# State additions between convolution taps, gate projections cut in halves, step sizes by 128-column weights

## The chip, the cores and the metric

The kernel runs on one core of a Trainium2 chip. The metric is the device time of one execution in microseconds (us). Engines are named as in the profile: PE (TensorE matmuls), PEld (its weight loads), DVE (VectorE), ACT (ScalarE), POOL (GpSimd), SP (the queue that issues DMAs). Each engine works through its own queue strictly in order.

## The reference, cut to what matters

One layer on 512 latent tokens and 256 context tokens, with D = 1024 and 32-bit inputs. Two branches read the same normalized input `h`: a retention branch with four heads, and a state-space branch (SSD) with eight groups of four heads.

```
xbc = silu(dwconv_centred(xbc, conv_w, conv_b))          # five taps over time
xs, bm, cm = split(xbc)
dt = softplus(dt_raw + dt_bias)                          # step sizes, 64 columns of h @ w_in
a  = dt * -exp(a_log)
# per direction, chunk by chunk, starting from the context's final state:
y  = q.S * exp(cumsum a) + intra-chunk part
S' = exp(sum a) * S + sum_j k_j (to_end * v_j)           # "fade" and "gain"
ys = (y + D*xs) * silu(z)                                # z: a gate projection
out = (sigmoid(g_r) * o_ret + sigmoid(g_s) * o_ssd) @ w_out
```

## The kernel before, in words

All projections are 32-bit products made of three passes (`mm3`): input and weight are each split into a high part (`hh`, `whi`) and a residue (`hl`, `wlo`), and high x high, residue x high and high x residue are added in PSUM. A weight unit (128 x 1024, eight contraction tiles of 128 columns) is loaded by SP, cast by ACT (`cast`, or L126 in `wunit`) and its residue taken by DVE (`rest`, or L127).

The kernel has four stages: modulation and normalization (to about 76 us), retention (to about 500 us), the state-space branch (to about 985 us), and the output projections.

**Retention** is ordered by a scheduler. For each head: queries, keys and values (`qkv`), `attention`, a gate projection (`gproj`), a norm, and `finish` (transposes at L418, products with the gate at L420). Between the values of head 1 and `finish` of head 0 the step sizes are computed (`stepsizes`): a projection of 64 columns onto 512 and then 256 tokens, copied from PSUM by ACT, then a long run of DVE steps (softplus, cumulative sums, decays). Those DVE steps stand in DVE's queue among the score products of head 1's attention (`a` at L368, its residue `al` at L155, which PE needs at L380).

**The state-space branch** is written in a fixed order. Eight groups overlap: while group g is scanned (`cur`), group g+1's inputs are projected (`job`), so the loop starts at g = -1 with projections alone. A group has six slots, one weight unit each: s = 0 to 3 are convolution inputs (x0, x1, B, C), s = 4 and 5 are the two gate projections (z). In slot s PE runs the projection of this slot while DVE applies the convolution of the job of the slot before (`prev.taps`, four products with `scalar_tensor_tensor` at L645 behind a first tap on ACT, then `prev.finish` at L650). The scan of the current group is woven in:

- `turn`, `turned`: transposes of x and B on PE (L725), their copies on ACT, weighted values `vw` on DVE (L740). Tiles 4 and 5 are the context, in slot 4; tiles 0 and 3 follow in slot 5.
- `context_state` (slot 5): the context's state, on PE (L746), copied by ACT.
- `fade(i)` (POOL, L765) multiplies a state by its decay, `gain(i)` (PE, L755) makes what one chunk adds, and `gained(i)` (DVE, L759) adds the two. So the states are a chain: fade(0), gained(0), fade(1), gained(1), fade(2), gained(2).
- `readers` (POOL, L794), `exponents` (POOL, L777), `choose` (DVE, L781), `weigh` (DVE, L789): the scan's decay factors.
- `outputs(0)` at the start of slot 3, `outputs(1)` at the start of slot 4 (PE, L808) read the four states. `merge` (DVE, L816 and L817) takes their results.

Of the kernel before, what the change touches and what calls it, by code (L numbers as in the profile page):

```python
# [7 lines left out]
F32 = mybir.dt.float32  # L8
# [57 lines left out]
def hybrid_layer_kernel(ctx: ExitStack, tc: tile.TileContext, x, xc, vec, tab, msk, w_mod, bgate, npost,  # L66
# [63 lines left out]
    def mm3(ps, pairs):  # L130

        n = len(pairs)
        for i, (a, b) in enumerate(pairs):
            ah, al = a
            bh, bl = b
            nc.tensor.matmul(ps, ah, bh, start=(i == 0), stop=False)  # L136
            nc.tensor.matmul(ps, ah, bl, start=False, stop=False)  # L137
            nc.tensor.matmul(ps, al, bh, start=False, stop=(i == n - 1))  # L138
# [132 lines left out]
    with ExitStack() as st:  # L271
# [151 lines left out]
        def stepsizes():  # L423
# [3 lines left out]
            wk = projw(wunit(w_dt), 64)  # L427
            u = t("dtu")
            ps = bank([64, LT])
            proj(ps, wk, 0, LT)  # L430
            nc.scalar.copy(u[0:64, :], ps[:, 0:384])
            nc.scalar.copy(u[64:128, 0:128], ps[:, 384:512])
            ps = bank([64, LC])
            proj(ps, wk, LT, LC)
            nc.scalar.copy(u[64:128, 128:384], ps)
# [13 lines left out]
            m = t("dtm")  # L449
# [135 lines left out]
    with ExitStack() as st:  # L585
# [25 lines left out]
        class Conv:  # L611
# [27 lines left out]
            def taps(self):  # L639
# [4 lines left out]
                for i in range(1, 5):  # L644
                    nc.vector.scalar_tensor_tensor(acc, raw[:, i:i + n], col(w0 + i), acc, ALU.mult, ALU.add)  # L645
# [6 lines left out]
        class Gate:  # L652
# [5 lines left out]
            def mm(self, wk, part):  # L658
                if part == 0:
                    self.pa = pbank("pr", 3)  # L660
                    proj(self.pa, wk, 0, LT)
# [14 lines left out]

            def finish(self):
                pass

        class Late:  # L680


            def __init__(self, job):
                self.early = self.taps = self.finish = lambda: None
# [160 lines left out]
        def slot(s, t, job, prev, old, cur, nxt):  # L845
# [14 lines left out]
            elif s == 1:  # L860
# [7 lines left out]
                call(cur, ("readers", 1), ("decay", 2), ("gained", 1), ("fade", 2), ("decay", 3))  # L868
                rest(t + 2)
                prev.finish()  # L870
                call(cur, ("weigh", 2), ("weigh", 3))
            elif s == 2:
# [7 lines left out]
                call(cur, ("readers", 2), ("readers", 3), ("gained", 2))  # L880
                rest(t + 2)
                prev.finish()
            elif s == 3:
# [5 lines left out]
                cast(t + 2)  # L889
                rest(t + 2)  # L890
                prev.finish()
                call(old, ("totalled",))
            elif s == 4:
                call(cur, ("outputs", 1))
                prev.early()
                call(nxt, ("open",), ("turn", 4, 5))
                job.mm(w, 0)
                prev.taps()
                cast(t + 2)
# [4 lines left out]
            elif s == 5:  # L904
                prev.early()
                call(nxt, ("context_state",))
                job.mm(w, 0)
# [5 lines left out]
            else:  # L913
                prev.early()
                job.mm(w, 0)
                cast(t + 2)
# [284 lines left out]
```

## Time and profile before

| | us |
|---|---|
| median of three timed runs | 1286.09 (1284.51 to 1289.94) |
| profiled execution, its own time | 1284.94 |
| span of that execution | 1283.2 |

The profiled execution lies 1.15 us under the median, and 1.74 us of it lie outside the span. By engine, PE has matmuls in flight in 96% of the span and DVE is busy in 63%; but DVE's share is an average over unequal stages: in slices 17 to 30 of 40, which is the state-space branch, it is 70 to 90% and more, while it is mostly 20 to 70% elsewhere. A matmul's listed duration covers its way through the array, so back-to-back matmuls overlap and the distance between starts is what each costs. PE's idle time is therefore read from the waits and from stretches, not from the busy sum.

### The profile page before, as it was taken

Reading aid. Unit: us, or ns where it says so; the run is one execution under the profiler, and the core shown is the slowest. Engines: PE = TensorE matmul, PEld = TensorE weight load, DVE = VectorE, ACT = ScalarE, POOL = GpSimd, SP = SyncE. Lnnn points to the kernel's source line nnn. Section 1 sums busy time; section 2 is a strip of 40 time slices with the busy share of each in tenths; the row PEclk is TensorE's granted clock in tenths of the full one; section 3 lists DMA queues with packets and bytes.
Section 4 is the critical chain, followed back from the end, with each engine's and each line's share of the span. In section 5 each row is a group of like instructions: output and inputs, shape, how many; then the busy total and the mean of one; then the engine's idle time right before and its main releaser. Section 6 shows DMA issues by size and latency. Waiting matters only on the chain.

```text
span 1283.2 us, 16075 instructions
## 1 busy us (share of the span) xinstructions
PE 1232.5 (96%) x6415; PEld 1011.7 (79%) x6415; DVE 814.5 (63%) x951; ACT 436.8 (34%) x694; POOL 335.4 (26%) x272
## 2 busy tenths in 40 slices
PE   5899999899999999999999999999999999999997
PEld 1588888688888888788888878787878888888876
DVE  1774442963454254879998998998984347344543
ACT  2533232233323212434344434344333443222221
POOL 0330110101011000365554756574553200000000
PEclk9899999999999999999999999999999999999999
DMA  8431122122202214315253442525153466345521
GB/s 311 171 96 48 66 66 66 54 79 79 82 33 82 66 50 156 147 50 199 72 190 112 151 156 95 188 72 197 54 210 99 156 205 215 115 147 164 203 93 65
DMA packets 43100, 155.92 MB, mean 122 GB/s; under 512 B 5097, under 2 KB 5897, under 8 KB 37906
## 3 DMA queue, kind: packets, MB, share of 16 engines
q1 hardware_dynamic: 42322, 152.77, 34.5%
q0 software_dynamic: 704, 2.13, 0.7%
q8 instruction: 50, 0.82, 0.3%
q14 instruction: 24, 0.20, 0.1%
HBM read 144.10 MB, written 10.78 MB: 121 GB/s over the span
## 4 chain that ended last, share of the span: by engine, by line
PE 80%; DVE 12%; issue 2%; ACT 1%; DMA 0%; DVEq 0%; POOLq 0%; ACTq 0%
PE pj L136 12%; PE pj L138 11%; PE pj L137 11%; PE pb L342 7%; PE pr L136 7%; DVE cacc L645 6%; PE pr L138 6%; PE pr L137 6%; PE py L808 4%; PE pj L342 3%; PE pj L1072 2%; PE pb L1072 2%; PE pb L380 2%; PE pb L378 1%; PE pb L379 1%
## 5 line engine op out<-in xcount | busy, mean ns | idle before, releaser
L136 PE MATMUL pr<-hh,whi 128*128 128x512 f32 (+1 forms) x640 | 240.2, 375 | 0.0
L138 PE MATMUL pr<-hh,wlo 128*128 128x512 f32 (+1 forms) x640 | 229.6, 359 | 0.0
L137 PE MATMUL pr<-hl,whi 128*128 128x512 f32 (+1 forms) x640 | 229.3, 358 | 0.0
L127 DVE TENSOR_TENSOR wlo<-wraw,whi 128x1024 fp32r<-128x1024 f32 x89 | 108.8, 1223 | 165.8 <-ACT whi L126 165.6
L126 ACT CAST whi<-wraw 128x1024 fp32r<-128x1024 f32 x89 | 93.7, 1053 | 247.3 <-PE pj L137 155.6
L645 DVE SCALAR_TENSOR_TENSOR cacc<-raw,vt,cacc 128x772 f32<-128x772 f32 x96 | 138.6, 1444 | 11.3 <-ACT cacc L643 7.8
L136 PE MATMUL pj<-hh,whi 128*128 128x512 f32 (+3 forms) x384 | 142.2, 370 | 0.0
L138 PE MATMUL pj<-hh,wlo 128*128 128x512 f32 (+3 forms) x384 | 142.1, 370 | 0.0
L137 PE MATMUL pj<-hl,whi 128*128 128x512 f32 (+3 forms) x384 | 142.1, 370 | 0.0
L136 PEld LDWEIGHTS pr<-hh,whi 128*128 128x128 f32 x640 | 121.1, 189 | 20.1 <-issue 3.5
L137 PEld LDWEIGHTS pr<-hl,whi 128*128 128x128 f32 x640 | 121.2, 189 | 18.7 <-issue 1.9
L138 PEld LDWEIGHTS pr<-hh,wlo 128*128 128x128 f32 x640 | 121.0, 189 | 18.3
L777 POOL TENSOR_TENSOR rows<-rows,ctok 128x512 f32<-128x512 f32 x64 | 89.5, 1420 | 108.5 <-DMA rows<-rows_d 105.2
L794 POOL TENSOR_TENSOR rows<-c,rows 128x512 f32<-128x512 f32 x64 | 112.5, 1782 | 0.0
L559 DVE TENSOR_TENSOR wlo<-wraw,whi 128x1024 fp32r<-128x1024 f32 x56 | 89.2, 1594 | 19.2 <-ACT whi L552 19.2
L137 PE MATMUL pj<-ul,whi 128*128 128x512 f32 x256 | 100.7, 393 | 0.0
L136 PE MATMUL pj<-uh,whi 128*128 128x512 f32 x256 | 100.7, 393 | 0.0
L138 PE MATMUL pj<-uh,wlo 128*128 128x512 f32 x256 | 100.6, 393 | 0.0
L136 PEld LDWEIGHTS pj<-hh,whi 128*128 128x128 f32 (+1 forms) x384 | 71.7, 187 | 13.2 <-issue 0.2
L138 PEld LDWEIGHTS pj<-hh,wlo 128*128 128x128 f32 (+1 forms) x384 | 71.8, 187 | 12.9
L137 PEld LDWEIGHTS pj<-hl,whi 128*128 128x128 f32 (+1 forms) x384 | 71.6, 187 | 12.9
L649 ACT ACTIVATE cth<-cacc 128x772 f32<-128x772 f32 (+1 forms) x32 | 25.4, 795 | 146.9 <-DVE cacc L645 146.9
(280 smaller groups left out, 2178.5 us busy)
## 6 DMA issues: line engine op xcount, KB each, us to landing
rows<-rows_d SPq DMA_DIRECT2D x32, 1024.0 KB, 7.5
wmod<-in_w_mod_dram SPq DMA_DIRECT2D x8, 1024.0 KB, 8.7
wraw<-in_w_v_dram SPq DMA_DIRECT2D x16, 512.0 KB, 3.5
wraw<-in_w_g_dram SPq DMA_DIRECT2D x16, 512.0 KB
wraw<-in_w_xs_dram SPq DMA_DIRECT2D x16, 512.0 KB, 3.5
wraw<-in_w_z_dram SPq DMA_DIRECT2D x16, 512.0 KB, 3.4
wraw<-in_w_gt_dram SPq DMA_DIRECT2D x16, 512.0 KB, 3.7
uraw<-u_d SPq DMA_DIRECT2D x32, 256.0 KB, 3.6
```

Source lines behind the costliest of these rows:

```text
L126: nc.scalar.copy(hi, raw)
L127: (eng or nc.vector).tensor_tensor(lo, raw, hi.bitcast(F32), ALU.subtract)
L136: nc.tensor.matmul(ps, ah, bh, start=(i == 0), stop=False)
L137: nc.tensor.matmul(ps, ah, bl, start=False, stop=False)
L138: nc.tensor.matmul(ps, al, bh, start=False, stop=(i == n - 1))
L342: nc.tensor.matmul(pv[i], a[:, k, sl], wv[b][:, k2, :], start=(k == 0 and j == 0), stop=(k == KT - 1 and j == 2))
L559: nc.vector.tensor_tensor(lo, r, hi.bitcast(F32), ALU.subtract)
L645: nc.vector.scalar_tensor_tensor(acc, raw[:, i:i + n], col(w0 + i), acc, ALU.mult, ALU.add)
L777: nc.gpsimd.tensor_tensor(v64(rows[:, d, :]), v64(rows[:, d, :]), bc(cb, 3, 64), ALU.add)
L794: nc.gpsimd.tensor_tensor(rows[:, 2 + d, :], self.c2, rows[:, 2 + d, :], ALU.mult)
L808: nc.tensor.matmul(py[64 * q:64 * q + 64, sl], lhs, rhs, start=(term == 0), stop=(term == 2))
L1072: nc.tensor.matmul(pss[e], mg[k][a][:, sl], wo[k][b][:, ec], start=(k == 0 and j == 0), stop=(k == KT - 1 and j == 2))
```

## The change

Three edits.

1. `taps` is cut in two: `taps` issues taps 1 and 2, the new `taps2` taps 3 and 4. In slots 1 and 2 `gained(1)` and `gained(2)` now stand on DVE between the two halves. In slots 3 and 4 both halves follow each other as before, with `cast` on ACT between them in slot 3.
2. The gate projections of slots 4 and 5 (and of the last stretch) are issued as two halves of four contraction tiles each, in one PSUM accumulation. In slot 4 the first half stands ahead of the context's transposes, in slot 5 ahead of `context_state`; the second half stands behind.
3. `stepsizes` puts the high part and the residue of its 64 columns side by side as one 128-column weight. Two passes (with `hh` and `hl`) replace three; the two halves of the result are copied apart by six ACT copies instead of three and added on DVE. The cast and the residue cover 512 columns instead of 1024.

```diff
-            wk = projw(wunit(w_dt), 64)
+            nc.scalar.copy(bv[:, :, 0:64], rv)
+            nc.vector.tensor_tensor(bv[:, :, 64:128], rv, bv[:, :, 0:64].bitcast(F32), ALU.subtract)
             u = t("dtu")
-            ps = bank([64, LT])
-            proj(ps, wk, 0, LT)
-            nc.scalar.copy(u[0:64, :], ps[:, 0:384])
-            nc.scalar.copy(u[64:128, 0:128], ps[:, 384:512])
-            ps = bank([64, LC])
-            proj(ps, wk, LT, LC)
-            nc.scalar.copy(u[64:128, 128:384], ps)
+            u2 = t("dtm")
+            for t0, n, parts in ((0, LT, ((0, 0, 384, 0), (64, 384, 512, 0))), (LT, LC, ((64, 0, LC, 128),))):
+                ps = bank([P, n])
+                for k in range(KT):
+                    for h in (hh, hl):
+                        nc.tensor.matmul(ps, bv[:, k, :], h[:, k, t0:t0 + n], start=(k == 0 and h is hh),
+                                         stop=(k == KT - 1 and h is hl))
+                for p0, a0, a1, c0 in parts:
+                    nc.scalar.copy(u[p0:p0 + 64, c0:c0 + a1 - a0], ps[0:64, a0:a1])
+                    nc.scalar.copy(u2[p0:p0 + 64, c0:c0 + a1 - a0], ps[64:128, a0:a1])
+            nc.vector.tensor_tensor(u, u, u2, ALU.add)
...
-                for i in range(1, 5):
+                for i in range(1, 3):
+                    nc.vector.scalar_tensor_tensor(acc, raw[:, i:i + n], col(w0 + i), acc, ALU.mult, ALU.add)
+
+            def taps2(self):
+                n, raw, acc, w0 = self.n, self.raw, self.acc, V_CW + self.ctile * 5
+                for i in range(3, 5):
                     nc.vector.scalar_tensor_tensor(acc, raw[:, i:i + n], col(w0 + i), acc, ALU.mult, ALU.add)
...
             def mm(self, wk, part):
                 if part == 0:
                     self.pa = pbank("pr", 3)
-                    proj(self.pa, wk, 0, LT)
+                half = slice(4 * part, 4 * part + 4)
+                mm3(self.pa, list(zip(wk, hsl(0, LT)))[half], part == 0, part == 1)
...
                 call(cur, ("readers", 1), ("decay", 2), ("gained", 1), ("fade", 2), ("decay", 3))
+                prev.taps2()
                 rest(t + 2)
...
                 call(cur, ("readers", 2), ("readers", 3), ("gained", 2))
+                prev.taps2()
                 rest(t + 2)
...
                 prev.early()
+                job.mm(w, 0)
                 call(nxt, ("open",), ("turn", 4, 5))
-                job.mm(w, 0)
+                job.mm(w, 1)
...
                 prev.early()
+                job.mm(w, 0)
                 call(nxt, ("context_state",))
-                job.mm(w, 0)
+                job.mm(w, 1)
```

DVE in slots 1 and 2 of one group, before (`cacc` is the convolution, `st` the state with `tk` from PE, `wlo` the residue of a weight unit, `rows` the decay factors):

```order
L740 TENSOR_TENSOR vw<-tk,wtok 128x512 x2
L645 SCALAR_TENSOR_TENSOR cacc<-raw_3645,vt,cacc 128x772 x4
L759 TENSOR_TENSOR st_4388<-st_4388,tk 128x512
L559 TENSOR_TENSOR wlo<-wraw,whi 128x1024
L650 SCALAR_TENSOR_TENSOR x_4509<-cth,cacc 128x772
L789 TENSOR_TENSOR rows<-rows,sc 128x512 x2
L645 SCALAR_TENSOR_TENSOR cacc<-raw_3646,vt,cacc 128x772 x4
L759 TENSOR_TENSOR st_4389<-st_4389,tk 128x512
```

The same place after:

```order
L759 TENSOR_TENSOR vw<-tk,wtok 128x512 x2
L656 SCALAR_TENSOR_TENSOR cacc<-raw_3632,vt,cacc 128x772 x2
L778 TENSOR_TENSOR st_4388<-st_4388,tk 128x512
L661 SCALAR_TENSOR_TENSOR cacc<-raw_3632,vt,cacc 128x772 x2
L570 TENSOR_TENSOR wlo<-wraw,whi 128x1024
L666 SCALAR_TENSOR_TENSOR x_4496<-cth,cacc 128x772
L808 TENSOR_TENSOR rows<-rows,sc 128x512 x2
L656 SCALAR_TENSOR_TENSOR cacc<-raw_3633,vt,cacc 128x772 x2
L778 TENSOR_TENSOR st_4389<-st_4389,tk 128x512
L661 SCALAR_TENSOR_TENSOR cacc<-raw_3633,vt,cacc 128x772 x2
```

Each state addition has moved ahead of two of the four taps of its slot; the number of instructions is the same.

PE in slot 4 of the first pass (g = -1), before, around the context's transposes (`tk<-ident`); the 24 matmuls of the gate follow them:

```order
L138 MATMUL pr<-hh,wlo 128x512
L725 MATMUL tk<-ident,x_3668 128x128 x2
L725 MATMUL tk<-ident,b_3669 128x128
L725 MATMUL tk<-ident,x_3668 128x128 x2
L725 MATMUL tk<-ident,b_3669 128x128
L136 MATMUL pr<-hh,whi 128x512
```

After, the rows read alike, but the twelve matmuls ahead of the transposes belong to the gate itself:

```order
L138 MATMUL pr<-hh,wlo 128x512
L744 MATMUL tk<-ident,x_3655 128x128 x2
L744 MATMUL tk<-ident,b_3656 128x128
L744 MATMUL tk<-ident,x_3655 128x128 x2
L744 MATMUL tk<-ident,b_3656 128x128
L136 MATMUL pr<-hh,whi 128x512
...
L138 MATMUL pr<-hh,wlo 128x512
L765 MATMUL tk<-vw,btok 128x512 x2
L136 MATMUL pr<-hh,whi 128x512
```

24 matmuls stand between the transposes and the context's state (L765), as before; now they are the second half of slot 4 and the first half of slot 5.

DVE in the attention of head 1, before, around the cumulative sums (`cum`) of the step sizes; `a` is a score product, `al` its residue:

```order
L368 TENSOR_TENSOR a<-pj,ec 128x512
L447 TENSOR_SCALAR dtu<-dt,dta 128x384
L458 SCALAR_TENSOR_TENSOR cum<-dtm,dtu 32x384 x2
...
L492 TENSOR_TENSOR rest<-tot,cum 128x384
L155 TENSOR_TENSOR al<-a,ah 128x512
L494 TENSOR_TENSOR ew<-rest,toend 128x384
L395 BN_STATS s_2033<-pb 128x6
```

After:

```order
L155 TENSOR_TENSOR al<-a,ah 128x512
L458 TENSOR_SCALAR dtu<-dt,dta 128x384
L469 SCALAR_TENSOR_TENSOR cum<-dtm,dtu 32x384 x2
...
L503 TENSOR_TENSOR rest<-tot,cum 128x384
L368 TENSOR_TENSOR a<-pj,ec 128x512
L505 TENSOR_TENSOR ew<-rest,toend 128x384
L155 TENSOR_TENSOR al<-a,ah 128x512
```

The last score product `a` of head 1 has moved from ahead of the cumulative sums to behind them, and its residue stands one step later.

## Rows read from the trace of the kernel before

**Rows 1.** Busy time by engine: busy us (share of the span), instructions.

```profile
PE 1232.5 (96%) x6415; PEld 1011.7 (79%) x6415; DVE 814.5 (63%) x951; ACT 436.8 (34%) x694; POOL 335.4 (26%) x272
```

**Rows 2.** Stretches of one period each: length, busy PE PEld DVE ACT POOL, granted clock, DMA.

```profile
541.76:596.59 54.83, 54.83 (x355) 46.62 (x355) 42.90 (x45) 21.98 (x38) 27.94 (x21) 1.00 0.37 132
...
596.59:654.09 57.50, 55.25 (x357) 46.71 (x357) 53.81 (x50) 23.94 (x42) 34.59 (x25) 1.00 0.38 137
654.09:713.15 59.06, 56.89 (x358) 48.38 (x357) 53.97 (x49) 23.93 (x42) 32.63 (x24) 0.97 0.39 133
...
sum 348.09, PE 334.77 PEld 283.55 DVE 320.17 ACT 143.53 POOL 203.08; mean PE 55.80 PEld 47.26 DVE 53.36 ACT 23.92 POOL 33.85
```

**Rows 3.** Waits, 596.59 to 944.68: us in total, times, longest; PEld's, then DVE's.

```profile
PEld py L808 <- DVE st L759: 14.8, 6, 2.5
...
DVE cacc L645 <- ACT cacc L643: 12.4, 6, 3.2
DVE st L759 <- PE tk L755: 11.8, 6, 3.9
```

**Rows 4.** Timeline of PE at outputs(0): start, us, instruction, [idle before <- releaser].

```profile
634.04 0.44 PE L808 MATMUL py<-rows,st 128*64 128x128 f32 x4
636.73 0.44 PE L808 MATMUL py<-rows,st 128*64 128x128 f32 x4 [2.25 <-DVE st L759]
```

**Rows 5.** Stretches around the ends of two waits: same columns as rows 2.

```profile
694.00:699.00 5.00, 4.87 (x47) 4.61 (x48) 4.81 (x6) 3.07 (x5) 0.00 (x0) 0.66 0.35 108
...
534.20:537.20 3.00, 2.92 (x9) 2.54 (x10) 2.53 (x5) 1.54 (x4) 0.00 (x0) 0.51 0.55 175
```

**Rows 6.** Timeline of DVE in slots 0 to 2.

```profile
562.87 4.18 DVE L645 SCALAR_TENSOR_TENSOR cacc<-raw,vt,cacc 128x772 f32<-128x772 f32 x4
...
614.26 2.29 DVE L559 TENSOR_TENSOR wlo<-wraw,whi 128x1024 fp32r<-128x1024 f32 x1
...
625.07 1.22 DVE L559 TENSOR_TENSOR wlo<-wraw,whi 128x1024 fp32r<-128x1024 f32 x1
...
628.70 7.37 DVE L645 SCALAR_TENSOR_TENSOR cacc<-raw,vt,cacc 128x772 f32<-128x772 f32 x4
636.00 0.68 DVE L759 TENSOR_TENSOR st<-st,tk 128x512 f32<-128x512 f32 x1
```

**Rows 7.** Chain that ended last, slot 1: start, us, engine, tile, line.

```profile
617.76 1.78 DVE cacc L645
619.57 1.96 DVE cacc L645
...
623.53 1.03 DVE cacc L645
```

**Rows 8.** Timeline of PE: gain(1) in group 0 and in group 1.

```profile
565.74 1.03 PE L755 MATMUL tk<-vw,btok 128*128 128x256 f32 x4
...
620.55 1.02 PE L755 MATMUL tk<-vw,btok 128*128 128x256 f32 x4
```

**Rows 9.** Timeline of POOL in the same slots.

```profile
618.67 4.00 POOL L794 TENSOR_TENSOR rows<-c,rows 128x512 f32<-128x512 f32 x2
625.23 2.84 POOL L765 TENSOR_TENSOR st<-st,etb 128x256 f32<-128x256 f32 x2 [2.55 <-DVE st L759]
```

**Rows 10.** Chain that ended last: twelve matmuls of 512 columns in a row.

```profile
81.51 2.72 PE pj L342 x12
```

**Rows 11.** Timeline of PE in slot 4 of the first pass.

```profile
534.28 0.48 PE L725 MATMUL tk<-ident,b 128*128 128x128 f32 x1 [3.17 <-DVE b L650]
```

**Rows 12.** Stretches of the step sizes' projection, PE alone: length, busy (instructions), clock, DMA.

```profile
215.19:220.70 5.51, 5.51 (x25) 1.00 0.25 82
220.70:223.44 2.74, 2.74 (x25) 1.00 0.07 27
```

**Rows 13.** Timeline of PE in the attention of head 1.

```profile
257.38 2.07 PE L380 MATMUL pb<-vh,al 128*128 128x512 f32 x4 [5.46 <-DVE al L155]
```

**Rows 14.** Timeline of DVE: the start of the stretch ahead of that.

```profile
224.08 1.41 DVE L420 SCALAR_TENSOR_TENSOR u<-pj,vt,g 128x512 f32<-128x512 f32 x2 [5.90 <-PE pj L418]
```

More of the change, by code (lines that the diff above doesn't have):

```diff
@@ L128, in wunit, with mm3 @@
         return hi, lo
-    def mm3(ps, pairs):
+    def mm3(ps, pairs, first=True, last=True):
         n = len(pairs)
@@ L135, in mm3 @@
             bh, bl = b
-            nc.tensor.matmul(ps, ah, bh, start=(i == 0), stop=False)
+            nc.tensor.matmul(ps, ah, bh, start=(first and i == 0), stop=False)
             nc.tensor.matmul(ps, ah, bl, start=False, stop=False)
-            nc.tensor.matmul(ps, al, bh, start=False, stop=(i == n - 1))
+            nc.tensor.matmul(ps, al, bh, start=False, stop=(last and i == n - 1))
     def projw(w, n=P):
@@ L426, in stepsizes @@
             t = lambda n, w=384: sp.tile([P, w], F32, name=n, tag=n)
-            wk = projw(wunit(w_dt), 64)
-            u = t("dtu")
-            ps = bank([64, LT])
-            proj(ps, wk, 0, LT)
-            nc.scalar.copy(u[0:64, :], ps[:, 0:384])
-            nc.scalar.copy(u[64:128, 0:128], ps[:, 384:512])
-            ps = bank([64, LC])
-            proj(ps, wk, LT, LC)
-            nc.scalar.copy(u[64:128, 128:384], ps)
+            raw = wp.tile([P, UNIT], F32, name="wraw", tag="wraw")
+            nc.sync.dma_start(raw, w_dt)
+            both = wp.tile([P, UNIT], F32R, name="whi", tag="whi")
+            bv = both.rearrange("p (k c) -> p k c", k=KT)
+            rv = raw.rearrange("p (k c) -> p k c", k=KT)[:, :, 0:64]
+            nc.scalar.copy(bv[:, :, 0:64], rv)
+            nc.vector.tensor_tensor(bv[:, :, 64:128], rv, bv[:, :, 0:64].bitcast(F32), ALU.subtract)
+            u = t("dtu")
+            u2 = t("dtm")
[9 more added lines that the diff above has]
+            nc.vector.tensor_tensor(u, u, u2, ALU.add)
             e = t("dte")
@@ L447, in stepsizes @@
             nc.vector.tensor_scalar(a, dt, av, None, ALU.mult)
-            m = t("dtm")
+            m = u2
             nc.gpsimd.memset(m, 1.0)
@@ L675, in taps @@
                 pass
+            taps2 = taps
             def finish(self):
@@ L683, in __init__ @@
             def __init__(self, job):
-                self.early = self.taps = self.finish = lambda: None
+                self.early = self.taps = self.taps2 = self.finish = lambda: None
         def group_jobs(g):
@@ L889, in slot @@
                 cast(t + 2)
+                prev.taps2()
                 rest(t + 2)
@@ L895, in slot @@
                 prev.early()
+                job.mm(w, 0)
                 call(nxt, ("open",), ("turn", 4, 5))
-                job.mm(w, 0)
+                job.mm(w, 1)
                 prev.taps()
+                prev.taps2()
                 cast(t + 2)
@@ L915, in slot @@
                 job.mm(w, 0)
+                job.mm(w, 1)
                 cast(t + 2)
```

## The prediction, made before the changed kernel ran

> **What bounds the kernel now.** I read the page first: PE has matmuls in flight in 96% of the span [rows 1], so a saving must shorten PE's work or close one of its gaps. The wait lists give the gaps. After the start-up three are worth naming, and the change touches each: the state-space loop's outputs(0), the context's transposes of the first pass, and head 1's attention.
>
> *The loop.* Stretches from one context state (L746) to the next are the loop's period [rows 2]. The first, of group 0, takes 54.83 us and PE is busy throughout. The six that follow take 348.09 us, 58.0 on average; two are printed, and of the six four lie near 57.5 and two near 59.1. In each PE waits once, at outputs(0), for the last state addition on DVE: 14.8 us in six waits, 2.47 each [rows 3], seen at 636.73, 2.7 us behind the first four matmuls of the same line [rows 4]. Without it a period of 57.50 would be 55.03. That is a floor: group 0 has two matmuls less and takes 54.83. The two long periods show half clock behind that wait (0.66 granted over 5 us [rows 5]) and lose 59.06 - 57.50 = 1.56 more.
>
> *Why DVE is late there.* DVE is busy 53.36 of 58.0 us per period and idles 12.4 and 11.8 us over the six, waiting for ACT at the C convolution and for PE at gained(0) [rows 2, 3]. So DVE has room on average, but its order is wrong: gained(2) starts at 636.00, behind four taps that began at 628.70 [rows 6], while PE stands at outputs(0) from 634.04 [rows 4]. PE waits for DVE, and DVE later waits for the PE that it held up.
>
> **The change, part by part.**
>
> **State additions between taps.** No instruction is added. gained(2) moves ahead of half of four taps that took 7.30 us (628.70 to 636.00), so it starts near 632.35 and ends near 632.95. PE needs it at about 634.3 (634.04 and four matmuls). That is 1.3 us to spare. Two things eat into it. First, gained(1) moves ahead of two taps too and may meet gain(1) unfinished: taps 1 and 2 of slot 1 end at 617.76 + 1.78 + 1.96 = 621.5 [rows 7], gain(1) ends at 621.57 [rows 8], a wait of 0.1. Behind it on DVE stand taps 3 and 4, the residue, the finish and all of slot 2; ACT's tanh and PE's outputs wait for those. Second, fade(2) and the products behind it on POOL are released about 3 us earlier, and then run beside DVE work that had POOL idle: the fourth tap of slot 1 took 1.03 where its neighbours took 1.96 beside POOL's L794 [rows 7, 9], and the residue behind it took 1.22 where another took 2.29 [rows 6]. That is 0 to 0.93 + 1.07 = 2.0 us ahead of gained(2); in exchange POOL is done earlier and later taps go free. I take half, which leaves the 1.3 us just positive, and charge 0.2 us of wait per period (bounds 0 and 0.7).
>
> The Trainium skill (page "SBUF — State Buffer", section "Who interferes with whom") speaks against this edit: a DVE instruction with two SBUF inputs and a GpSimd instruction that reads SBUF exclude each other, and the later one is blocked until the other has finished. A tap is such an instruction. By that rule a tap could wait for a whole L794 of 2.00 us and take 3.03. The traced taps beside L794 take 1.96, so the trace shows the blocking but a smaller price, and the sum goes by 1.96.
>
> **Gate halves.** In the steady loop the twelve matmuls ahead of the transposes delay them by 2.72 us [rows 10], but without the outputs(0) wait PE gets there 2.47 earlier, so ACT's copies, DVE's vw and POOL's fade(0) see them as now. The cover is DVE's queue: vw stands behind the C taps. With both kinds of earliness the next place to be late is gain(0), which needs vw of tiles 0 and 3. DVE now waits 11.8/6 = 1.97 us on average at gained(0), just behind that, and gets 12.4/6 = 2.07 earlier if PE no longer holds it up at the C taps; PE arrives 2.47 earlier. So the mean period has room, the tightest may not; I charge 0.2 (bounds 0 and 0.7). Loop: 55.03 + 0.4 = 55.43 per period, six take 332.6: **-15.5** (bounds: 55.03 gives -17.9; 56.43 gives -9.5).
>
> In the first pass nothing is scanned yet, and the transposes wait 3.17 us for B's finish [rows 11]. The first half now fills 2.72 of it. PE then ran at the lower clock, 1.2 of 2.4 GHz (0.51 over 3 us [rows 5]), a loss of about 1.3 us which a wait of 0.4 should not cause: **-4.0** (bounds -2.6, if the clock falls all the same, and -4.4). Group 0 behind it has a DVE that is idle 12 of 55 us [rows 2], so this arrives.
>
> **Step sizes.** The projection runs 24 matmuls of 512 columns in 5.51 us and 24 of 256 in 2.74 [rows 12], 0.23 and 0.114 each, with weights of 64 columns; with 128-column weights twelve of 512 take 2.72 [rows 10], 0.227 each, so the wider weight costs nothing. Sixteen of each remain: 8 x 0.23 + 8 x 0.114 = 2.75 us less on PE. It does not all arrive. From 224.08 DVE, which waited for PE's transposes, works until the last residue of the scores, for which PE waits 5.46 us, to 257.38 [rows 13, 14]: this stretch belongs to DVE. DVE starts 2.75 earlier, but carries one addition of 384 columns more (some 0.55, by the 0.68 of 512 columns [rows 6]) and one such step ahead of the residue (0.55). The last score product now stands behind the cumulative sums as well, so all twelve of the last value matmuls wait and not four: PE resumes some 2.3 us earlier (257.38 to 255.1, at the cast behind that product) with 24 matmuls of that gate projection and the values to do instead of 17, 7 x 0.23 = 1.6. Net **-0.7** (bounds: -2.75 if all of it arrives, +1.8 if DVE's stretch gains nothing). The six ACT copies replace three beside PE work, the halved cast and residue likewise; POOL's fill of the mask moves from the start to behind the addition, into an idle POOL.
>
> **Sum.** -15.5 - 4.0 - 0.7 = -20.2. On the profiled execution's 1284.94 that is 1264.7; on the median of 1286.09, 1265.9. I say **1266**. With all lower bounds (-25.0) the profile gives 1260, with all upper ones (-10.3) the median gives 1276.
>
> **Rivals.**
>
> *The port takes half of it.* If POOL's earlier start costs DVE the full 2.0 us per period and no later tap is freed, DVE is busy 55.4 and keeps a wait or two of 0.7; a period takes about 56.9. The loop gives 6.7, with the rest 11.4: **1274** (1271 to 1279). For it: every tap beside POOL doubles [rows 7]. Against it: POOL's work is the same, and what it blocks earlier it does not block later. With blocking in full, by the page above, DVE would carry some 57.4 and the whole come to about 1278, in the same case.
>
> *The wait only moves.* The edit does what it says at outputs(0), but PE then waits the same 2.5 us at gain(0) or at the context state, because DVE's 58 us per period were its own. Only the first pass and the step sizes stay: -4.7, **1281**. Against it: DVE idles 4.0 us per period [rows 3].
>
> *Slower: gained(1) stalls DVE.* In group 0 DVE reaches that point early: taps 1 and 2 end near 562.87 + 2.1 = 565.0, gain(1) ends at 566.8 [rows 6, 8], a new wait of 1.8 us with two taps, residue and finish behind it. If each of six periods has this wait, and the port's 2.0 on top, and the old idle 4.0 remains, a period takes 53.36 + 4.03 + 1.8 + 2.0 = 61.2: +19 in the loop, **1301** in all. It decides from a period of 59.9. Against it: in group 1 the wait is 0.1, since DVE is later there.
>
> **How the numbers follow.** A change under 0.5% (6.4 us) is about what a measurement of this kernel cannot tell from none. Forecast 0.60, port 0.20, wait moved 0.13, slower 0.07. The range takes in the forecast's bounds and the port's case: 1260 to 1279, some 0.78. Faster by over 0.5% (under 1279.7): forecast and port, 0.80; within: 0.13; slower: 0.07.
>
> **What would show it.** Right: the six periods near 55.4, no wait of L808 over 1 us and no half clock behind it, the first pass's transposes waiting under 1 us, DVE busy about 53 per period; in head 1's attention a wait of PE of about 5 us that has moved to the first value products. Wrong: L808 still waiting, DVE busy over 55 per period with taps 3 and 4 of slot 1 at 1.96, or a new wait at L755 or L746.

## The result, and the profile of the changed kernel

| | us | ratio to the kernel before, 95% interval |
|---|---|---|
| before, first comparison | 1286.3 | |
| changed kernel, median of four | 1268.5 (1265.67 to 1270.31) | 0.9856 [0.9828, 0.9885] |
| before, second comparison | 1287.18 | |
| changed kernel, second comparison, five runs | 1268.03 (1265.27 to 1269.15) | 0.9851 [0.9835, 0.9867] |

The change is faster by 1.4 to 1.5%. The profiled execution of the changed kernel took 1270.31 us with a span of 1268.5, the slowest of its four. To see where the 14.7 us between the two spans went, both traces are cut at the starts of the same matmuls. The last piece runs to the end of the last PE instruction; group 0's context state stands twelve matmuls (2.72 us, [rows 10]) later in PE's order after the change, so the third piece and the last one are shown with 2.72 moved back.

| piece | before | after | difference | predicted |
|---|---|---|---|---|
| start to the step sizes' projection | 215.19 | 217.17 | +1.98 | 0 |
| from there to the transposes of head 3's `finish` | 283.10 | 280.56 | -2.54 | -0.7 |
| to the first context state | 43.31 | 41.98 | -1.33, less 2.72: -4.05 | -4.0 |
| period of group 0 | 54.82 | 54.83 | 0 | 0 |
| six periods | 348.09 | 332.78 | -15.31 | -15.5 |
| last group and tail | 335.52 | 338.06 | +2.54, plus 2.72: +5.26 | 0 |

The first row is not the change's. PE issues nothing of it there (only the cast and the residue of edit 3 run in that time, on ACT and DVE), and the 1.98 us are all there by PE's first product with `hh`, which starts at 40.75 before and at 42.72 after. From that product to the projection it is 174.4 to 174.5 us in all thirteen traces of this study, while the projection itself starts anywhere between 214.73 and 217.86. Two rows fit, one is larger than predicted, and the last one, a loss, was in no term.

The page's first part, busy time by engine, answers [rows 1]: PE lost 3.4 us of busy time, the rest was gaps.

```profile
PE 1229.1 (97%) x6399; PEld 1008.6 (80%) x6399; DVE 814.9 (64%) x952; ACT 437.9 (35%) x697; POOL 339.3 (27%) x272
```

The stretches of the six periods (columns as in [rows 2]) and the waits within them, PEld's and then DVE's (us in total, times, longest):

```profile
594.70:650.44 55.74, 55.32 (x358) 46.68 (x357) 53.42 (x50) 24.05 (x42) 34.97 (x26) 1.00 0.39 142
...
705.92:760.96 55.04, 55.04 (x357) 46.74 (x357) 51.24 (x49) 23.82 (x42) 34.62 (x24) 1.00 0.39 144
...
sum 332.78, PE 331.36 PEld 280.17 DVE 319.13 ACT 143.52 POOL 206.95; mean PE 55.23 PEld 46.70 DVE 53.19 ACT 23.92 POOL 34.49
```

```profile
PEld py L827 <- issue: 4.9, 12, 0.5
...
PEld tk L774 <- DVE vw L759: 3.1, 4, 0.9
```

```profile
DVE st L778 <- PE tk L774: 6.1, 12, 2.5
DVE cacc L656 <- ACT cacc L654: 5.0, 7, 0.7
```

The six waits of 2.47 us at outputs(0) [rows 3] are gone: L827, which was L808, waits for no state any more. DVE's own idle time at the taps, for the first tap on ACT, fell from 12.4 to 5.0 us and at the additions from 11.8 to 6.1. What PE still waits for is gain(0) (L774), in four periods of six, for the weighted values of tiles 0 and 3 (`vw`).

DVE's timeline in slots 1 and 2 of group 1 shows the new order, two taps, addition, two taps:

```profile
613.74 3.84 DVE L656 SCALAR_TENSOR_TENSOR cacc<-raw,vt,cacc 128x772 f32<-128x772 f32 x2
617.73 0.69 DVE L778 TENSOR_TENSOR st<-st,tk 128x512 f32<-128x512 f32 x1 [0.15 <-PE tk L774]
618.34 2.52 DVE L661 SCALAR_TENSOR_TENSOR cacc<-raw,vt,cacc 128x772 f32<-128x772 f32 x2
...
625.53 4.11 DVE L656 SCALAR_TENSOR_TENSOR cacc<-raw,vt,cacc 128x772 f32<-128x772 f32 x2
629.56 0.68 DVE L778 TENSOR_TENSOR st<-st,tk 128x512 f32<-128x512 f32 x1
630.16 2.07 DVE L661 SCALAR_TENSOR_TENSOR cacc<-raw,vt,cacc 128x772 f32<-128x772 f32 x2
```

gained(1) waits 0.15 for PE (predicted 0.1). Taps 1 and 2 now take 1.9 to 2.05 each on average and taps 3 and 4 1.03 to 1.26. The eight taps of these two slots sum to 12.5 us where they took 14.2, but the residue and the finish behind slot 1's taps grew from 1.22 and 1.39 to 1.64 and 2.06: what is stretched beside POOL has moved, and DVE's busy time per period stayed (53.36 before, 53.19 now).

In the last group PE's and DVE's timelines show the loss. `vw` (L759) starts on DVE at 938.82, behind a weight residue (L570); PE stood at gain(0) 3.04 us for it, and the matmuls behind it take 0.63 instead of 0.39. The stretch behind it had a granted clock of 0.50, which is the lower of the two levels, 1.2 GHz.

```profile
939.29 2.08 PE L774 MATMUL tk<-vw,btok 128*128 128x256 f32 x4 [3.04 <-DVE vw L759]
940.80 0.99 PE L136 MATMUL pr<-hh,whi 128*128 128x512 f32 x1
941.59 0.63 PE L137 MATMUL pr<-hl,whi 128*128 128x512 f32 x1
```

```profile
936.00 2.30 DVE L570 TENSOR_TENSOR wlo<-wraw,whi 128x1024 fp32r<-128x1024 f32 x1
938.23 0.68 DVE L687 SCALAR_TENSOR_TENSOR z<-cth,pr 128x512 f32<-128x512 f32 x1
938.82 0.74 DVE L759 TENSOR_TENSOR vw<-tk,wtok 128x256 f32<-128x256 f32 x2
```

```profile
939.20:944.70 5.50, 5.41 (x13) 4.32 (x14) 4.23 (x8) 0.00 (x0) 2.46 (x3) 0.50 0.30 95
```

In head 1's attention PE's 5.46 us for the last residue [rows 13] became 4.02 at the first value product of that tile, ending at 255.57, which is 38.40 us behind the start of the projection; before it was 257.38 - 215.19 = 42.19.

```profile
255.57 0.50 PE L378 MATMUL pb<-vh,ah 128*128 128x512 f32 x1 [4.02 <-ACT ah L154]
```

That is 3.8 us earlier, where the prediction had 2.3. DVE's and POOL's timelines tell why. Before, the two first cumulative sums and the copy behind them took 2.85 and 1.08 us while POOL wrote the context decays of the next head (`ec`, L355):

```profile
246.77 2.85 DVE L458 TENSOR_TENSOR_SCAN cum<-dtm,dtu 32x384 f32<-32x384 f32 x2
249.66 1.08 DVE L459 COPY tot<-cum 32x6 f32<-32x6 f32 x1
```

```profile
246.83 3.88 POOL L355 TENSOR_TENSOR ec<-strip 128x512 f32<-128x512 f32 x2 [64.38 <-ACT strip L351]
```

After, POOL waits for the last score product, which reads `ec` and has moved behind the sums, and these take 1.93 and 0.16, which is 1.84 less. The write now stands beside that tile's residue, which takes 1.41 instead of 0.68, so part of its price now falls behind PE's resumption instead of ahead of it:

```profile
246.08 1.93 DVE L469 TENSOR_TENSOR_SCAN cum<-dtm,dtu 32x384 f32<-32x384 f32 x2
248.03 0.16 DVE L470 COPY tot<-cum 32x6 f32<-32x6 f32 x1
...
255.55 1.41 DVE L155 TENSOR_TENSOR al<-a,ah 128x512 fp32r<-128x512 f32 x1 [0.28 <-ACT ah L154]
```

```profile
254.99 3.11 POOL L355 TENSOR_TENSOR ec<-strip 128x512 f32<-128x512 f32 x2 [29.09 <-DVE a L368]
```

### The profile page after: what moved, and what is told of

Same layout as the page of the kernel before. It is cut to its first block, busy times and chain, and to the rows that moved or that the text cites. A ratio compares the mean times of both kernels' runs of the same rounds, so it can differ in the third digit from the quotient of the medians.

```text
span 1268.5 us, 16050 instructions
## 1 busy us (share of the span) xinstructions
PE 1229.1 (97%) x6399; PEld 1008.6 (80%) x6399; DVE 814.9 (64%) x952; ACT 437.9 (35%) x697; POOL 339.3 (27%) x272
## 4 chain that ended last, share of the span: by engine, by line
PE 82%; DVE 9%; issue 2%; ACT 2%; DMA 0%; DVEq 0%; POOLq 0%; ACTq 0%
PE pj L136 11%; PE pj L137 11%; PE pj L138 11%; PE pr L136 7%; PE pr L138 7%; PE pr L137 7%; PE pb L342 7%; PE pj L342 3%; PE py L827 3%; PE pj L1098 2%; PE pb L1098 2%; PE tk L774 2%; DVE cacc L656 2%; PE pb L380 2%; DVE cacc L661 2%
## 5 line engine op out<-in xcount | busy, mean ns | idle before, releaser
L136 PE MATMUL pj<-hh,whi 128*128 128x512 f32 (+1 forms) x368 | 136.8, 372 | 0.0
L137 PE MATMUL pj<-hl,whi 128*128 128x512 f32 (+1 forms) x368 | 136.6, 371 | 0.0
L138 PE MATMUL pj<-hh,wlo 128*128 128x512 f32 (+1 forms) x368 | 136.6, 371 | 0.0
L796 POOL TENSOR_TENSOR rows<-rows,ctok 128x512 f32<-128x512 f32 x64 | 93.1, 1477 | 102.1 <-DMA rows<-rows_d 102.0
L813 POOL TENSOR_TENSOR rows<-c,rows 128x512 f32<-128x512 f32 x64 | 116.0, 1836 | 0.0
L570 DVE TENSOR_TENSOR wlo<-wraw,whi 128x1024 fp32r<-128x1024 f32 x56 | 90.5, 1615 | 22.2 <-ACT whi L563 22.2
L656 DVE SCALAR_TENSOR_TENSOR cacc<-raw,vt,cacc 128x772 f32<-128x772 f32 x48 | 75.1, 1565 | 13.4 <-ACT cacc L654 12.5
L136 PEld LDWEIGHTS pj<-hh,whi 128*128 128x128 f32 x368 | 69.4, 189 | 12.3 <-issue 0.2
L138 PEld LDWEIGHTS pj<-hh,wlo 128*128 128x128 f32 x368 | 69.4, 188 | 12.0
L137 PEld LDWEIGHTS pj<-hl,whi 128*128 128x128 f32 x368 | 69.4, 189 | 12.0
```

The costliest lines, as they stand in the source:

```text
L136: nc.tensor.matmul(ps, ah, bh, start=(first and i == 0), stop=False)
L138: nc.tensor.matmul(ps, al, bh, start=False, stop=(last and i == n - 1))
L570: nc.vector.tensor_tensor(lo, r, hi.bitcast(F32), ALU.subtract)
L796: nc.gpsimd.tensor_tensor(v64(rows[:, d, :]), v64(rows[:, d, :]), bc(cb, 3, 64), ALU.add)
L813: nc.gpsimd.tensor_tensor(rows[:, 2 + d, :], self.c2, rows[:, 2 + d, :], ALU.mult)
```

## The experiments

Eleven runs followed, one of them of the changed kernel again, each against the kernel before on its own chip. The pieces are cut as above, each from the one trace of its run; "last" holds the landmark, so that 332.8 (335.52 - 2.72) is no loss where the gates are halved.

| kernel | median us | ratio | steps to head 3 | to context state | six periods | last |
|---|---|---|---|---|---|---|
| before | 1286 to 1287 | | 283.10 | 43.31 | 348.09 | 335.52 |
| changed | 1268.5 | 0.9856 | 280.56 | 41.98 | 332.78 | 338.06 |
| changed, again | 1268.03 | 0.9851 [0.9835, 0.9867] | 280.66 | 41.95 | 332.69 | 336.77 |
| e1 additions alone | 1273.59 | 0.9898 [0.9884, 0.9911] | 284.14 | 43.56 | 333.93 | 335.71 |
| e2 halves alone | 1281.77 | 0.9959 [0.9947, 0.9970] | 283.24 | 41.97 | 348.14 | 331.89 |
| e3 step sizes alone | 1282.21 | 0.9969 [0.9956, 0.9982] | 281.45 | 43.50 | 347.95 | 335.51 |
| e4 changed, last gates whole | 1265.67 | 0.9835 [0.9823, 0.9848] | 280.70 | 41.97 | 334.66 | 333.41 |
| e5 e4, values ahead of residue | 1261.22 | 0.9798 [0.9780, 0.9816] | 280.43 | 41.98 | 330.48 | 332.79 |
| e6 second addition alone | 1271.66 | 0.9881 [0.9862, 0.9900] | 284.25 | 43.57 | 333.57 | 335.71 |
| e7 e3, two `ec` buffers | 1285.74 | 0.9987 [0.9977, 0.9998] | 283.20 | 43.07 | 348.10 | 335.50 |
| e8 e4, step sizes cut late | 1263.51 | 0.9816 [0.9797, 0.9835] | 279.18 | 41.95 | 333.79 | 332.79 |
| e10 e5, step sizes cut early | 1254.01 | 0.9744 [0.9730, 0.9757] | 273.88 | 42.13 | 330.32 | 332.79 |
| e11 changed, values ahead | 1262.54 | 0.9809 [0.9795, 0.9822] | 281.74 | 41.97 | 330.42 | 333.85 |

### e1: the additions between the taps, alone

The kernel before with the diff's edit 1 and nothing else.

> The kernel before with the state additions between the taps alone. My theory (the wait of 2.47 us at outputs(0) goes, and nothing replaces it because the gate halves are not there to delay the transposes and the context state): the six periods fall from 348.1 to about 331, no half clock behind outputs(0), wait at gain(0) 0; whole kernel about 17 us under the kernel before, ratio 0.987. Rival 1 (the additions only help together with the gate halves; alone the wait moves to gain(0) or to the context state): periods 340 or more, ratio 0.995 to 1. Rival 2 (GpSimd beside the taps costs DVE 2 us per period): DVE busy 55 per period, periods near 57, ratio 0.995.

Measured 13 us, ratio 0.9898, and six periods of 333.93: my theory, less 3 to 4 us. The additions carry the loop's gain by themselves. The waits of PEld in the six periods, with no line for outputs(0) any more:

```profile
PEld tk L732 <- DVE b L655: 3.3, 6, 0.6
...
PEld tk L753 <- DVE vw L747: 1.5, 6, 0.2
PEld tk L762 <- DVE vw L747: 1.4, 4, 0.4
```

Without the halves PE meets B's finish too early at the context's transposes (L732), and its weight loads also wait a little at the context state (L753) and at gain(0) (L762). These waits of PEld sum to 6.2 us; what arrives in the time is 0.6 us per period, 333.93 / 6 = 55.66 over the 55.05 of the changed kernel's best. The waits stand in another place than in the changed kernel, where I had expected none.

### e2: the gate halves, alone

The kernel before with the diff's edit 2 and nothing else.

> The kernel before with the gate projections in halves alone. My theory: the first pass gains 4.0 us (up to the context state of group 0, of which 2.7 us is only the place of the landmark), the six periods keep the wait at outputs(0) and stay at 348 or rise a little because the transposes and the context state stand 2.7 us later; in the last group, where the last stretch's gates are cut as well, gain(0) has 12 matmuls ahead of it instead of 24 and PE waits about 3 us there and then runs at the lower clock: 5 us lost against the landmark. Sum about 0 to +2, ratio 1.000 to 1.002. Rival (the halves carry a part of what the loop gained): periods 340 or less, ratio 0.990.

The first pass gained as expected (43.31 to 41.97, plus the landmark: 4.1 us) and the six periods stayed at 348.14, with the same six waits:

```profile
PEld py L809 <- DVE st L760: 14.8, 6, 2.5
```

But the last group lost nothing (331.89, where 332.8 is even), so the whole came to a gain of 5 us and not to 0. The halves around gain(0) there are not enough for the wait of 3 us: it shows only with the additions too. In e2 the last group's `vw` starts on DVE 5.9 us behind the context state and PE asks for it 8.8 us behind it; in the changed kernel it starts 11.5 and 11.7 us behind it, in the kernel before 12.5 where PE, with the full gates ahead, asks at 14.2. Of the 5.6 us between e2 and the changed kernel, 1.7 are there when DVE begins C's finish. The other 3.9 lie in the steps from there to `vw`, the same in both kernels, which take 8.2 us in e2 and 12.1 in the changed kernel, as in the kernel before. Half of that is in the two predicated copies, shown below from e2 and then from the changed kernel; most of the rest is in two residues (1.22 and 1.34 against 2.08 and 2.30):

```profile
946.88 1.38 DVE L782 COPY_PREDICATED rows<-maskL,rows 128x512 f32<-128x512 uint32 x2
```

```profile
932.78 3.32 DVE L800 COPY_PREDICATED rows<-maskL,rows 128x512 f32<-128x512 uint32 x2
```

In e2 these copies and residues run undisturbed, at 0.69 and 1.22 to 1.34 each. Over the six periods, too, the same DVE instructions take 304.96 us in e2 and 320.17 in the kernel before, 2.5 us less per period. I read this as DVE being further ahead in e2, where PE still waits 2.5 us at each outputs(0), and so meeting POOL otherwise; no run tries that by itself. What is shown is that the loss in the last group comes only with both edits together. The medians say the same, less sharply: the three edits alone save 13.1, 5.0 and 4.5 us, 22.6 in all, and together 17.8 and 19.2 in the two comparisons.

### e3 and e7: the step sizes, alone, and with the next head's decays released early

e3 is the kernel before with the diff's edit 3. e7 adds a second buffer:

```diff
-            ec = r1.tile([P, 2, LT], F32, name="ec", tag="ec")
+            ec = r1.tile([P, 2, LT], F32, name="ec", tag="ec", bufs=2)
```

> The kernel before with the step sizes as two passes of 128 columns alone. The prediction on record gives 0.7 us (2.75 less on PE, of which DVE's stretch behind it keeps most). What the trace of the changed kernel shows by landmarks is 2.5 us; my theory for the difference is GpSimd's L355, which in the kernel before stood beside two cumulative sums on DVE (2.85 and 1.08 us instead of 1.93 and 0.16) and is now released behind them. Theory: 2.5 us less up to the end of retention, the cumulative sums at 1.93 and 0.16, ratio 0.998. Rival (the 2.5 us were drift of the start or of other stages): 0.7 us or nothing, ratio 0.9995 to 1.

> The step sizes alone, with two buffers for the context decay that GpSimd writes for the next head (L355), so that it need not wait for the last score product of head 1 and falls beside DVE's cumulative sums again, as in the kernel before. The step sizes alone gave 1282.2 us, with those sums at 1.93 (two) and 0.16. My theory (that GpSimd write cost the kernel before some 1.8 us on DVE in front of the residue that PE waits for, and its later release is the larger part of what I had not counted): two sums take 2.8 to 2.9 again or the sum and the copy behind it are stretched by 1.5 to 1.9 us in all, PE resumes that much later, whole kernel 1283.5 to 1284. Rival (the operations do not disturb one another, the earlier figures had another cause): sums of 1.93 beside it, 1282.

e3 saves 4.5 us by its median (0.9969, interval 2.3 to 5.7 us), 1.65 by its trace up to head 3, where the changed kernel shows 2.54 and 2.44. So 0.7 was too little, which e3's interval excludes, and my 2.5 was not reached in this trace. The sums and the copy take 1.93 and 0.16, as expected. The spread between these traces fits the lower clock behind PE's wait of 4 us: ten matmuls are listed at 0.63 us behind it in e3 and five in the changed kernel.

e7 takes most of it back: 0.9987 against 0.9969, with intervals that just overlap, and 1.75 us by the traces (281.45 to 283.20), PE's wait 5.62 instead of 4.02. POOL's L355 runs at once when its input is there, now not beside the sums but beside the two steps ahead of them:

```profile
242.88 3.21 POOL L355 TENSOR_TENSOR ec<-strip 128x512 f32<-128x512 f32 x2 [18.65 <-ACT strip L351]
```

```profile
243.28 1.67 DVE L155 TENSOR_TENSOR al<-a,ah 128x512 fp32r<-128x512 f32 x1
244.87 1.44 DVE L458 TENSOR_SCALAR dtu<-dt,dta 128x384 f32<-128x384 f32 x1
246.42 1.93 DVE L469 TENSOR_TENSOR_SCAN cum<-dtm,dtu 32x384 f32<-32x384 f32 x2
```

In e3 these steps take 0.69 and 0.42, so the price is 2.0 us, in the size expected though on other instructions. The median is 1.7 to 2.2 us above what I had expected, on another chip than e3's. A buffer more, which only lets POOL start earlier, cost the path 1.75 us by the traces.

### e4, e11 and e5: the wait at gain(0)

e4 gives the last stretch's gates back in one piece; e11 moves the weighted values of tiles 0 and 3 on DVE (and ACT's copies) ahead of slot 5's residue; e5 does both. "Changed, again" is the unaltered changed kernel on e11's chip.

```diff
             def mm(self, wk, part):
                 if part == 0:
                     self.pa = pbank("pr", 3)
-                half = slice(4 * part, 4 * part + 4)
-                mm3(self.pa, list(zip(wk, hsl(0, LT)))[half], part == 0, part == 1)
+                    if not self.silu:
+                        proj(self.pa, wk, 0, LT)
+                if self.silu:
+                    half = slice(4 * part, 4 * part + 4)
+                    mm3(self.pa, list(zip(wk, hsl(0, LT)))[half], part == 0, part == 1)
```

```diff
-                call(cur, ("turned", 0, 3), ("scores",))
+                call(cur, ("scores",))
...
-                call(nxt, ("exponents", 3), ("choose", 0), ("choose", 1))
+                call(nxt, ("exponents", 3), ("choose", 0), ("choose", 1), ("turned", 0, 3))
                 rest(t + 2)
```

> The changed kernel, but the gates of the last stretch (slots 0 to 2 while the last group is scanned) are issued whole ahead of gain(0), gain(1) and gain(2) as in the kernel before; slots 4 and 5 keep their halves. My theory (the wait of 3.5 us at gain(0) of the last group comes from the 12 matmuls that no longer stand ahead of it, and the clock falls behind it): no wait over 0.8 us there, full clock, 4.5 to 5.3 us less than the changed kernel, about 1263.5 where that has 1268.5, ratio to the kernel before 0.982. Rival (DVE is simply late in the last group whatever stands there, and PE waits as long at the next need, outputs(0)): no gain, 1268, ratio 0.986.

> The changed kernel with only the weighted values of tiles 0 and 3 ahead of slot 5's residue; the last stretch's gates stay in halves around gain(0). Theory: the wait of 3.5 us at gain(0) of the last group has two parts, 2.3 us of residue ahead of the values on DVE and 2.7 us of matmuls taken out from ahead of gain(0); without the residue 1.2 us or less are left and the clock stays up, the loop falls to 330.5, so this alone gives 1261 to 1263, nearly what both give (1261.2). Rival (the halves in the last stretch cost in other places too, gain(1) and gain(2)): 1264 to 1265.

> The changed kernel with the last stretch's gates whole (1265.7 us median, six periods 334.7 in its trace, gain(0) waiting 5.3 us in them for the weighted values of tiles 0 and 3), and in addition these weighted values (with ACT's copies of the transposes) stand ahead of the weight residue of slot 5 on DVE, not behind it. My theory (what is left of a wait in the loop is that residue of 2.3 us ahead of them, not DVE's load as a whole): no wait at gain(0), periods 55.05 to 55.1, six 330.5, about 4 us less, 1262. Rival (DVE is now as busy as PE, so the wait only moves, to outputs(0) or the residue's own reader, the weights of slot 0): periods stay at 55.5 to 55.8, 1265 to 1266.

> The changed kernel as it is, on the chip of the other runs of this call, to set them against. 1266 to 1270 by its first runs; the last group's gain(0) waits 3.5 us again and the clock falls behind it (theory), or not (rival: that wait was an accident of one execution).

The unaltered kernel waits again (3.24 us at gain(0) of the last group, granted clock 0.73 behind it), so the wait was no accident. e4 closes it: PE waits 0.36 there, the last piece falls by 3.4 to 4.7 us to 333.41. Its median is only 2.4 to 2.8 under the changed kernel's, where I had expected 4.5 to 5.3, since its six periods are 1.9 longer in the trace (gain(0) waits in all six, 5.3 us; why in all six there is not known). e11 leaves 0.23 us of the wait at gain(0), and its six periods are 330.42. But the second row below is gain(1): there PE waits 1.11 us, for the values of tiles 1 and 2, which stand behind the next residue (2.31) on DVE, and it does not wait there in the changed kernel. So the rival that the halves cost elsewhere too holds in e11's mechanism, at 1.1 us (last piece 333.85 against e5's 332.79), while its time agrees with my theory. In e5 the loop has no wait of PE for DVE left: PE is busy for the whole stretch.

```profile
933.36 1.13 PE L774 MATMUL tk<-vw,btok 128*128 128x256 f32 x4 [0.23 <-DVE vw L759]
...
941.76 1.29 PE L774 MATMUL tk<-vw,btok 128*128 128x256 f32 x4 [1.11 <-DVE vw L759]
```

```profile
592.70:923.18 330.48, 330.48 (x2138) 280.34 (x2137) 319.45 (x295) 144.17 (x252) 207.25 (x145) 1.00 0.40 144
```

330.48 / 6 = 55.08 per period, within 0.05 of the floor of 55.03 that the prediction had worked out. DVE's busy time did not fall for it (319.45, 53.24 per period): the order ahead of gain(0) was what was left, not DVE's load. The rival that the wait would move on once more is refuted.

### e6: only the second addition

```diff
-                call(cur, ("readers", 1), ("decay", 2), ("gained", 1), ("fade", 2), ("decay", 3))
                 prev.taps2()
+                call(cur, ("readers", 1), ("decay", 2), ("gained", 1), ("fade", 2), ("decay", 3))
```

> The kernel before with only gained(2) moved between the taps of slot 2; gained(1) stays behind all four taps of slot 1. The additions alone gave six periods of 333.9 and 1273.6 us. My theory: only gained(2) is late for outputs(0); gained(1) behind the taps is in time for fade(2), so six periods are again 334 and the time 1273 to 1274. Rival 1 (the states are a chain, and gained(1) two taps later delays fade(2) on GpSimd, which stands behind readers, until gained(2) itself waits): periods of 56 to 57.5, 1280 or more. Rival 2 (moving gained(1) costs a wait of DVE for gain(1), as one of the prediction's cases had it): this kernel is faster than the additions alone by 0.15 to 1.8 us per period, 1263 to 1272.

Six periods of 333.57 against 333.93, and ratios whose intervals overlap: moving gained(1) gains nothing. The gain in the loop is gained(2) alone, the one that outputs(0) waits for. The median of 1271.66 lies at the edge of rival 2's range, but per period e6 is only 0.06 us faster, where that rival begins at 0.15. The cost that it names is in group 0, outside the six: there e1's gained(1) waits 1.93 us for PE, PE then 0.35 for B's finish, and the stretch is 0.76 longer than e6's. Below stand e1's row and then e6's:

```profile
544.62:599.92 55.30, 54.95 (x356) 46.58 (x354) 42.34 (x43) 21.78 (x38) 28.15 (x20) 1.00 0.35 126
```

```profile
545.68:600.22 54.54, 54.54 (x356) 46.64 (x354) 41.06 (x45) 22.01 (x38) 26.07 (x20) 1.00 0.37 130
```

### e8 and e10: where the step sizes' text is cut

The step sizes are emitted as a generator, and the retention stage's scheduler places what has been emitted. A further `yield` (with one more call for it) has the rest emitted behind head 2's inputs. e8, on e4, cuts ahead of the cumulative sums; e10, on e5, right behind the addition of the halves.

```diff
             nc.vector.tensor_tensor(u, u, u2, ALU.add)
+            yield
             e = t("dte")
...
-            if h < 2:
+            if h < 3:
                 next(steps)
```

> The changed kernel with the last stretch's gates whole (1265.7), and the step sizes' program text cut once more ahead of the cumulative sums, which are issued behind the inputs of head 2. In DVE's queue the last score product of head 1 then stands behind one cumulative sum and its residue behind three, where both stood behind all sums and the small copies. My theory (PE's wait of 4.0 us in head 1's attention and the lower clock behind it are only that order): PE resumes about 5 us earlier, the wait is under 1 us, 4 to 5.5 us less, 1260.5 to 1261.5. Rival (PE then waits elsewhere in heads 1 or 2 for the step sizes' remaining steps, or the time was not on the path): 1264 to 1266.

> The changed kernel with the last stretch's gates whole and the weighted values ahead of slot 5's residue (together 1261.2), and the step sizes cut right behind their addition, so that the scheduler places softplus and the cumulative sums behind head 1's score products where it can: in DVE's queue all six residues of head 1's attention now stand ahead of the first cumulative sum (cutting later, ahead of the cumulative sums, left PE a wait of 2.9 us and gave 2.2 us). My theory (PE's waits in head 1's attention, 1.8 for the banks and 4.0 for the last score product, with the lower clock behind, are all DVE's order): these waits under 1 us in all, no clock below 1 there, 5 to 7 us less, 1254.5 to 1256.5. Rival (the step sizes' DVE work must be paid somewhere in heads 1 and 2, and PE waits for it at the norm or at the next head's inputs): 1259 to 1261.

e8 missed half of its expectation: 2.2 us and a wait of 2.94 left. POOL's L355 is released early again by the earlier score product (the row names the copy at L471, which ends right behind that product) and falls beside a sum and the very residue PE waits for:

```profile
245.86 3.83 POOL L355 TENSOR_TENSOR ec<-strip 128x512 f32<-128x512 f32 x2 [21.87 <-DVE tot L471]
```

```profile
246.78 1.86 DVE L474 TENSOR_TENSOR_SCAN cum<-dtm,dtu 32x384 f32<-32x384 f32 x1
248.67 1.58 DVE L155 TENSOR_TENSOR al<-a,ah 128x512 fp32r<-128x512 f32 x1
```

A sum takes 0.95 alone (0.96 for the other ones in this trace) and the residue 0.69, so 1.8 us of the 2.94 are this. e10 has all six residues ahead of the sums. Of PE's waits there (1.8 and 4.0) one of 1.47 is left, where I had expected less than 1, the granted clock behind it is 1.00, and the piece up to head 3 falls from 280.43 to 273.88. The finish of head 1 comes 7.8 us earlier than in e5 and that of head 2 6.4, so head 2 gives back 1.4 of it. e10 is the best version of the study: 1254.0 us, 2.56% under the kernel before and 14 us under the changed one.

```profile
246.35 0.50 PE L380 MATMUL pb<-vh,al 128*128 128x512 f32 x1 [1.47 <-DVE al L155]
```

```profile
240.00:250.00 10.00, 8.53 (x38) 6.71 (x37) 9.90 (x18) 0.62 (x1) 2.98 (x2) 1.00 0.00 0
250.00:260.00 10.00, 10.00 (x46) 8.29 (x45) 8.70 (x15) 1.66 (x2) 1.95 (x2) 1.00 0.06 15
```

## Why the prediction was right, and where it was not

The time (1266 forecast, 1268.5 and 1268.0 measured) came out, with two errors of opposite sign in it; that the one hid between a third and a half of the other is luck.

- **Loop: right.** Six periods of 332.78 and 332.69, forecast 332.6. The wait at outputs(0) is gone, as e1 shows by itself and e6 narrows to gained(2). The floor of 55.03 is real (e5: 55.08). I had charged 0.4 us of new waits, half at outputs(0), half at gain(0); there are 55.46 - 55.05 = 0.4, all at gain(0). A new wait at L755, now L774, was named as a sign of being wrong; it came, at that size.
- **POOL beside the taps: right in the sum, wrong in one price.** The dear taps are now the first two and the cheap ones the last two, and DVE's busy time is that of the kernel before, so the rival of 56.9 us per period falls. DVE's busy time is not fixed, though: e2's is 2.5 us per period lower with the same instructions, and the sum had no term for that. POOL's products are stretched as well: L813, which was L794, takes 1.27 us at the shortest and 2.0 beside a tap (min, median and max of the line, in ns, below). A tap of 1.02 and a product thus share about 2.0 us, and a tap pays about 1 us for it.

```profile
L813 POOL TENSOR_TENSOR rows<-c,rows x64: 1267/2012/2288, 546.5 to 957.7; 128x512 f32<-128x512 f32 x64
```

  The prediction's 3.03 for a tap under full exclusion took the 2.00 of L794 as POOL's free time, and that already held POOL's own wait. The Trainium skill (page "SBUF — State Buffer", section "Who interferes with whom") says that such a pair excludes each other for a whole instruction. Read so, a tap and a product would take 1.02 + 1.27 = 2.29 us; the traces agree in kind, with 2.0.
- **gained(1) as a stall: right to price low.** In group 0 it does wait 1.94 us for PE, where 1.8 was named; in the six periods 0.15 to 0.17. Group 0's period stayed at 54.83 all the same; without the halves (e1) the stall does reach it, 55.30 against e6's 54.54.
- **First pass: right.** 4.05 and 4.08, forecast 4.0. The transposes still wait 0.45 us for B, and behind that the granted clock is 1.00.
- **Step sizes: mis-sized.** PE's own 2.75 is measured as 8.25 - 5.54 = 2.71. The term that failed is the resumption of PE, put 2.3 us earlier and in truth 3.8: I carried DVE's stretch over as it was, and 1.84 us of it were POOL's L355 beside the sums, which covers the 1.5 that were missing. POOL's queue was read only for the mask that the edit moves; that the edit also moves the last reader of `ec`, and with it POOL's next write, was not followed. Another 0.7 of the 2.5 is in head 2, where 0.45 us of a wait for a residue at 347.56 is gone; what moved that was not tried.
- **Last group: left out.** The halves also cut the last stretch's gates, which the change's description says, but no term priced it. gain(0) then has 12 matmuls (2.72) ahead of it instead of 24, while DVE's queue ahead of `vw` is the same and takes as long (12.1 us from C's finish on, in both). The tightest place in the loop had been charged 0.2 to 0.7 us from the mean idle time of the six periods; the last group, with less PE work in the slot, is none of them. It cost 5.26 and 3.97 us in the two traces, of which 3.0 and 3.2 are the wait and the rest fits the lower clock behind it. e1 and e2, which lose nothing there, show that it needs both edits, and e4 that it needs the cut of the last stretch's gates.

Against the forecast of -20.2 the step sizes gave 1.7 to 1.8 us more and the last group lost 4.0 to 5.3: the pieces that the change touches sum to -18.0 (again) and -16.6 (first trace). The start, which it does not touch, adds 0.5 and 2.0.

## What to carry to other kernels

When a wait disappears, ask at once who was ahead beside it: DVE was in time for the last group's shortened cover in e2, where PE still waited elsewhere, and late in the changed kernel, where the same DVE steps took 3.9 us longer. Walk an edit that cuts a helper through every caller, the prologue and the last iteration included, since these have other covers than the steady state. And a tile's last reader that moves takes the next writer with it: look at what that write will now run beside, above all POOL beside DVE.

## What the runs showed of the hardware that I had not expected

- A POOL write that was off every path cost the path 1.8 us in the kernel before: two cumulative sums and a 32x6 copy took 2.85 and 1.08 beside it, 1.93 and 0.16 alone. A copy of 0.16 took 0.92 more.
- The same DVE instructions took 304.96 us in six periods of e2 and 320.17 in the kernel before, 2.5 us per period more. The periods were equal all the same (348.14 and 348.09), since PE waited at outputs(0) in both.
- The lower clock behind a wait is not a fixed price. Behind much the same wait (3.04 and 3.24 us at gain(0), both in the last group) the granted clock over the next 5.5 us was 0.50 and 0.73; behind 4.02 us in head 1 the matmuls listed at 0.63 us numbered four or five in the changed kernel's traces, ten in e3's and twelve in e11's. Behind the waits of 1.11 (e11), 1.36 (changed kernel) and 1.47 (e10) none was slow. Part of what differs between traces of the same piece by 0.5 to 1.2 us fits this.
